# A transformer kernel on one core: the mixer's triangular inverse laid out for fewer block transposes, its elementwise work moved from GpSimd to VectorE, and a fixed queue place for one tile's transposes

## The chip, the cores and the metric

One core of a Trainium2 chip runs the whole program: TensorE (PE) does the matmuls, VectorE (DVE), ScalarE (ACT) and GpSimd (POOL) the work around them, and SyncE (SP) issues most of the transfers. The metric is the device time of one execution in microseconds (us). The kernel before was timed three times: 3140.81, 3150.64 and 3153.42 us, median 3150.64.

## The reference

The program is a stack of blocks over 512 tokens of width 1024, in float32. The change touches the first two: a hybrid mixer (a two-directional delta-rule scan over 8 heads, and a pooling branch) and a mixture over 16,384 experts (PEER). What follows them (two more attention mixers and two feed-forward layers) is untouched.

```python
def step(state, inp):                     # the scan, run forwards and backwards
    r_t, w_t, k_t, v_t, kk_t, a_t = inp
    sa = jnp.einsum('bhvk,bhk->bhv', state, -kk_t)
    state = (state * w_t[:, :, None, :]
             + sa[..., :, None] * (kk_t * a_t)[..., None, :]
             + v_t[..., :, None] * k_t[..., None, :])
    out = jnp.einsum('bhvk,bhk->bhv', state, r_t)
    return state, out

p = h @ w_in                              # the mixer: project, shift, scan, gate, pool, project
p_rw = bi_token_shift(p[..., :RWKV_IN], shift_mu)
...
y_pool = multiscale_pool(p_pool, pool_w, pool_scale)
return jnp.concatenate([y_rwkv, y_pool], axis=-1) @ w_out

ug = jnp.take(u_tab, idx, axis=0)         # the experts, for each token's 128 chosen rows
act = gelu(jnp.einsum('td,thkd->thk', xb, ug))
vg = jnp.take(v_tab, idx, axis=0)
return jnp.einsum('thk,thkd->td', gate * act, vg)
```

## The kernel before

**The mixer** (`mixer`, lines 1305 to 1484) takes roughly the first 508 us. Eight heads are worked as four pairs j = 0 to 3; a pair fills the 128 partitions, 64 for each head. The 512 tokens are cut into 8 chunks of 64, and inside a chunk the recurrence is solved in closed form: a strictly triangular 64x64 matrix is inverted for each chunk, head and direction. A pair goes through these steps:

- `keys`, `decay`, `queries` (lines 1589 to 1714) make the scaled operands: tiles `kk`, `sg`, `L`, `ta`, `b`, `BK`, `AR`, `kfs`. Much of it is elementwise on 128x512 (or 64x512) tiles, split between VectorE (`V`) and GpSimd (`G`).
- `grams` (from line 1715) multiplies them on TensorE and masks the products into `Ga` and `BG` (line 1739).
- `invert` (from line 1780) inverts the triangles. The 32x32 diagonal blocks are first transposed by VectorE into `W`, four transposes of 32 partitions each (line 1797). Then 15 rows of forward substitution run on VectorE, two small instructions for each row (lines 1810 and 1812), on all chunks at once. The 16x16 inverses and their transposes are scaled by ScalarE into `W` (line 1819) and brought back into `X` and `TT` by four transposes each (line 1824); `X` and `TT` were zeroed by GpSimd before. Two rounds of small matmuls (line 1834, results taken by lines 1842, 1847 and 1850) merge the blocks to 32 and 64.
- `solve`, `chain`, `tail` and `gate` form the outputs `y`.

The input projection runs as filler between these steps (`project`, tile `pp`): each pair of weight columns is loaded as `mraw`, and `split` turns it into two halves `mw`, one by a ScalarE cast and the other by a subtraction (lines 1524 and 1525), which goes to VectorE and to GpSimd by turns. The result is taken from PSUM and shifted by one ScalarE and two VectorE instructions (lines 1382 to 1385). The pooling branch adds on GpSimd, and the output projection splits its weights `ow` in the same way as `mw`.

The order comes from `timeline`: two tracks of pairs, (0, 2) and (1, 3), the second 69 units later, each step with a cost for each `yield`; the filler is placed behind the tracks' matmuls. A scheduler then orders each engine's instructions by when it takes them to be ready. Every engine runs its own queue in order.

**The experts.** Three of four token tiles meet all 128 expert columns densely: for each column a `pu` product of 24 matmuls and later a `pacc` sum of 18. Token tile 0 is instead worked from gathered rows (`chosen`): GpSimd issues an indirect transfer for each row and VectorE accumulates into `pe_acc` (line 634). When it is done, `end` (line 722) normalises tile 0 and `lay` (line 179) scales it into `xn` on VectorE (line 185) and transposes it on TensorE into `pf` (line 190), in the middle of the dense columns.

Of the kernel before, what the change touches and what calls it, by code (L numbers as in the profile page):

```python
# [23 lines left out]
S = 512  # L24
# [375 lines left out]
class Peer:  # L400
# [154 lines left out]
    def dense(self, wk, ps, hhi, hlo, early):  # L555
# [7 lines left out]
        def down(w, ahi, alo, i, t):  # L563
            l = [y[:, t * 128:(t + 1) * 128] for y in (ahi, alo)]
            for h in range(2):
                mm = k.mm3(acc[t][h], l, [y[:, h * 512:(h + 1) * 512] for y in w], i == 0, i == 127)
            return mm.ins
# [154 lines left out]
    def end(self, st, t, u, g, gpre, pool, ps):  # L722


        k, nc = self.k, self.k.nc
        V, A, G = nc.vector, nc.scalar, nc.gpsimd
        v = pool.tile([128, D], F32, name=k.name("v"), tag="v")
        y = pool.tile([128, D], F32, name=k.name("xn"), tag="xn")
        ms = k.small.tile([128, 2, 4], F32, name=k.name("ms"), tag="ems", bufs=2)
        for h in range(2):  # L730
            sl = slice(h * 512, (h + 1) * 512)
            d = V.tensor_tensor(out=v[:, sl], in0=u[:, sl], in1=g[:, sl], op=ALU.mult)
            for z, src in ((0, u), (1, v)):
                c = A.activation(y[:, sl], src[:, sl], AF.Square, scale=1.0 / 32.0, accum_out=ms[:, z, h:h + 1])
        st.marks.append((c.ins, d.ins))
        for _ in range(1 + 6 * (t == 0)):
            yield
        s = ms[:, :, 2]
        G.tensor_tensor(out=s, in0=ms[:, :, 0], in1=ms[:, :, 1], op=ALU.add)
        G.tensor_scalar(out=s[:, 0:1], in0=s[:, 0:1], scalar1=1e-5, scalar2=None, op0=ALU.add)  # L740
        G.tensor_scalar(out=ms[:, 0, 3:4], in0=s[:, 0:1], scalar1=1e-6, scalar2=None, op0=ALU.mult)
        G.tensor_tensor(out=s[:, 1:2], in0=s[:, 1:2], in1=ms[:, 0, 3:4], op=ALU.add)
        G.tensor_tensor(out=s, in0=s, in1=k.mhalf[:, 0:2], op=ALU.pow)
        st.lay(t, v, y, s[:, 1:2], gpre, lambda: ps.tile([128, 4, 128], F32, name=k.name("pf"), tag="pu"))
        A.activation(st.x[:, t, :], v, AF.Copy, scale=s[:, 0:1])
# [559 lines left out]
def mixer(k, ctx, xpool, a, ready):  # L1305
# [5 lines left out]
    with ExitStack() as psctx, ExitStack() as lctx:  # L1311
# [37 lines left out]
        with ExitStack() as rctx, ExitStack() as pctx:  # L1349
# [13 lines left out]
            def project(f, fin, tag="pj"):  # L1363

                p = ps.tile([128, 512], F32, name=k.name("pp"), tag=tag, bufs=1 if tag == "pj" else 3)
                for c2 in range(0, NC, 2):
# [3 lines left out]
                    split(k, raw, *w, eng=V if c2 % 4 else G)  # L1370
# [98 lines left out]
            for n, c in enumerate(order):  # L1469
                yz = part(late, 0, c, 2)  # L1470
                for h in range(2):
# [3 lines left out]
                    split(k, raw, *w, eng=G if h else V)  # L1475
# [11 lines left out]
def pool_branch(k, a, yp, col, rw, ps):  # L1487
# [7 lines left out]
    for gi, hw in enumerate(POOL_HALF):  # L1495
# [9 lines left out]
        for lv in range(gi + 1):  # L1505
            st = 1 << lv
            n -= st
            dst = q[lv % 2]
            G.tensor_tensor(out=dst[:, :n], in0=src[:, :n], in1=src[:, st:st + n], op=ALU.add)
            src = dst  # L1510
            yield
        m = rw.tl("db")
        G.tensor_tensor(out=m, in0=src[:, 16 - hw:16 - hw + S], in1=inv, op=ALU.mult)
# [41 lines left out]
class Rwkv:  # L1555
# [76 lines left out]
    def decay(self, j, d):  # L1632
# [26 lines left out]
        G.tensor_tensor(out=sg, in0=L, in1=sg, op=ALU.subtract)  # L1659
# [12 lines left out]
        else:  # L1672
            G.tensor_tensor(out=kfs, in0=kfs, in1=R(ta), op=ALU.add)
        G.tensor_tensor(out=ta, in0=ta, in1=R(kT), op=ALU.mult)
        yield
        BK = st["BK", d] = dt("BK", (128, 8, 2, 64))
        for h in range(2):
# [4 lines left out]
            G.tensor_tensor(out=BK[q, :, 1 - h, :], in0=ch(ta[q]), in1=ch(L[q]), op=ALU.mult)  # L1682
            yield

    def queries(self, j, d):
# [10 lines left out]
        G.tensor_tensor(out=AR[d][:, :, 1, :], in0=ch(R(r)), in1=e3, op=ALU.mult)  # L1696
        yield
        vd = v
        if d:
            vd = self.dt("sg")  # L1700
            G.tensor_copy(vd, v[:, ::-1])
# [13 lines left out]
    def grams(self, j, d):  # L1715
# [7 lines left out]
        if d == 0:  # L1723
            st["Ga"] = tl("Ga", (128, 2, 16, 64), 2)
        Ga = st["Ga"][:, :, 8 * d:8 * d + 8, :]
        msk = e.con("gmask").rearrange("p (s t) -> p s t", s=2)
        for c4 in range(2):
# [8 lines left out]
            for h in range(2):  # L1736
# [4 lines left out]
                yield  # L1741
        for c4 in range(2):
# [21 lines left out]
    def bonus(self, j):  # L1764
# [7 lines left out]
        G.tensor_tensor(out=kfs, in0=kfs, in1=r, op=ALU.mult)  # L1772
# [7 lines left out]
    def invert(self, j):  # L1780
# [9 lines left out]
        W = tl("W", (128, 16, 32))  # L1790
        P = tl("P", (128, 16, 64))
        tmp = P.rearrange("p a b -> p (a b)")
        Nn, Tt = (tmp[:, i * 256:(i + 1) * 256].rearrange("p (a b) -> p a b", a=16) for i in range(2))
        for h in range(2):
            for q in range(2):
                rows = slice(64 * h + 32 * q, 64 * h + 32 * q + 32)
                V.transpose(W[rows].rearrange("p a b -> p (a b)"),
                            Ga[rows, h, :, 32 * q:32 * q + 32].rearrange("p n (b t) -> p t b n", b=2))
                yield
# [14 lines left out]
        TT = tl("TT", (128, 16, 64))  # L1814
# [230 lines left out]
for _n, _c in (("blk", 128), ("gmask", 128), ("m16", 64), ("m32", 64), ("eye", 64), ("m01", 2), ("reset", 512)):  # L2045
# [25 lines left out]
def consts():  # L2071
# [10 lines left out]
    m["m01"] = np.stack([p % 32 < 16, p % 32 >= 16], 1)  # L2082
    m["reset"] = np.tile((np.arange(512) % 64 != 0)[None, :], (128, 1))
# [69 lines left out]
```

## Time and profile before

| what | value |
|---|---|
| median of three runs | 3150.64 us |
| the profiled execution | 3154.2 us, its span 3152.4 us |
| PE, DVE, ACT, POOL busy | 95%, 64%, 43%, 29% of the span |
| mean granted TensorE clock | 0.971 of full speed |

The span runs from the first to the last instruction. PE's share is the sum of modelled matmul times, so it is an upper figure. [...] The profile's share of POOL counts gathers in the expert stage too; the mixer is a sixth of the span.

### The profile page before, as it was taken

Reading aid. Unit: us, or ns where it says so; the run is one execution under the profiler, and the core shown is the slowest. Engines: PE = TensorE matmul, PEld = TensorE weight load, DVE = VectorE, ACT = ScalarE, POOL = GpSimd, SP = SyncE. Lnnn points to the kernel's source line nnn. Section 1 sums busy time; section 2 is a strip of 40 time slices with the busy share of each in tenths; the row PEclk is TensorE's granted clock in tenths of the full one; section 3 lists DMA queues with packets and bytes.
Section 4 is the critical chain, followed back from the end, with each engine's and each line's share of the span. In section 5 each row is a group of like instructions: output and inputs, shape, how many; then the busy total and the mean of one; then the engine's idle time right before and its main releaser. Section 6 shows DMA issues by size and latency. Waiting matters only on the chain. (4 is left out here: it accounts for less than half of the span.)

```text
span 3152.4 us, 45760 instructions
## 1 busy us (share of the span) xinstructions
PE 2982.1 (95%) x17602; PEld 2514.9 (80%) x17602; DVE 2030.4 (64%) x3837; ACT 1348.7 (43%) x2459; POOL 906.1 (29%) x662
## 2 busy tenths in 40 slices
PE   7888999998799999999998999989999899999999
PEld 5656668998688999999997987758888787888887
DVE  5767747998987888878887455665552343655522
ACT  5333334337733333333333355564442254544422
POOL 4322234630012544444443021212222331122221
PEclk9878999999999999999999999899999999999999
DMA  2000135234336999999997432313332332122322
GB/s 90 23 18 17 38 106 177 88 119 163 157 129 238 353 328 336 334 341 326 339 327 270 128 116 74 114 58 112 100 98 91 95 128 83 64 95 94 100 95 80
DMA packets 176202, 476.08 MB, mean 151 GB/s; under 512 B 18768, under 2 KB 68688, under 8 KB 175728
## 3 DMA queue, kind: packets, MB, share of 16 engines
q1 hardware_dynamic: 139120, 338.93, 31.8%
q0 software_dynamic: 36864, 134.23, 11.7%
q8 instruction: 138, 2.26, 0.3%
q14 instruction: 80, 0.66, 0.1%
HBM read 448.59 MB, written 24.51 MB: 150 GB/s over the span
## 5 line engine op out<-in xcount | busy, mean ns | idle before, releaser
L64 ACT CAST whi<-raw 128x1024 fp32r<-128x1024 f32 x494 | 518.1, 1050 | 712.2 <-PE pu L118 187.0
L67 DVE TENSOR_TENSOR wlo<-raw,whi 128x1024 fp32r<-128x1024 f32 x366 | 457.4, 1250 | 459.5 <-ACT whi L64 457.5
L67 POOL TENSOR_TENSOR wlo<-raw,whi 128x1024 fp32r<-128x1024 f32 x128 | 310.5, 2427 | 1085.6 <-ACT whi L64 994.3
L117 PE MATMUL pu<-pe_hhi,whi 128*128 128x384 f32 x1024 | 348.8, 341 | 2.3 <-ACT gl L545 1.7
L119 PE MATMUL pu<-pe_hhi,wlo 128*128 128x384 f32 x1024 | 347.2, 339 | 0.0
L118 PE MATMUL pu<-pe_hlo,whi 128*128 128x384 f32 x1024 | 347.1, 339 | 0.0
L118 PE MATMUL pacc<-wlo,ahi 128*128 128x512 f32 x768 | 303.3, 396 | 0.0
L117 PE MATMUL pacc<-whi,ahi 128*128 128x512 f32 x768 | 294.7, 396 | 3.1 <-ACT ahi L589 3.1
L119 PE MATMUL pacc<-whi,alo 128*128 128x512 f32 x768 | 290.7, 398 | 3.3 <-DVE alo L590 3.3
L119 PE MATMUL up<-res_h,wlo 128*128 128x512 f32 (+1 forms) x752 | 283.0, 377 | 1.0 <-DVE wlo L67 1.0
L117 PE MATMUL up<-res_h,whi 128*128 128x512 f32 (+1 forms) x752 | 283.5, 378 | 0.0
L118 PE MATMUL up<-res_h,whi 128*128 128x512 f32 (+1 forms) x752 | 283.4, 377 | 0.0
L253 DVE SCALAR_TENSOR_TENSOR u<-up,ffn_par,u 128x511 f32<-128x511 f32 (+1 forms) x176 | 131.4, 748 | 142.7 <-ACT u L251 139.6
L618 POOL DMA_INDIRECT row<-pe_v,pe_gs x128 | 165.6, 1294 | 199.4 <-DVE pe_acc L634 186.7
L618 POOL DMA_INDIRECT row<-pe_rows,pe_gs x128 | 167.0, 1305 | 189.2 <-DVE pe_gs L625 167.5
L117 PEld LDWEIGHTS pu<-pe_hhi,whi 128*128 128x128 f32 x1024 | 193.2, 189 | 7.6 <-ACT gl L545 2.0
L118 PEld LDWEIGHTS pu<-pe_hlo,whi 128*128 128x128 f32 x1024 | 193.2, 189 | 4.2
L119 PEld LDWEIGHTS pu<-pe_hhi,wlo 128*128 128x128 f32 x1024 | 192.9, 188 | 0.5
L119 PEld LDWEIGHTS pacc<-whi,alo 128*128 128x128 f32 x768 | 144.9, 189 | 38.1 <-DVE alo L590 3.8
L117 PEld LDWEIGHTS pacc<-whi,ahi 128*128 128x128 f32 x768 | 144.7, 189 | 33.4 <-ACT ahi L589 3.8
L118 PEld LDWEIGHTS pacc<-wlo,ahi 128*128 128x128 f32 x768 | 144.7, 188 | 30.9
L634 DVE SCALAR_TENSOR_TENSOR pe_acc<-row,pe_gs,pe_acc 128x1024 f32<-128x1024 f32 x128 | 163.7, 1279 | 4.0 <-DMA row<-pe_v,pe_gs 3.4
(502 smaller groups left out, 6460.2 us busy)
## 6 DMA issues: line engine op xcount, KB each, us to landing
raw<-pe_u SPq DMA_DIRECT2D x128, 512.0 KB, 5.5
raw<-pe_v SPq DMA_DIRECT2D x128, 512.0 KB, 5.8
raw<-ffn_up SPq DMA_DIRECT2D x88, 512.0 KB, 3.5
raw<-ffn_dn SPq DMA_DIRECT2D x44, 512.0 KB, 3.5
pe_gd<-go SPq DMA_DIRECT2D x24, 784.0 KB, 3.4
gc<-pe_gd SPq DMA_DIRECT2D x12, 1536.0 KB, 15.3
mraw<-mx_in SPq DMA_DIRECT2D x80, 128.0 KB, 2.2
raw<-pe_wq SPq DMA_DIRECT2D x16, 512.0 KB, 3.6
```

What stands on the lines that cost most here:

```text
L64: nc.scalar.copy(hi, raw)
L67: eng.tensor_tensor(out=lo, in0=raw, in1=hi, op=ALU.subtract)
L117: mm(out, l[0], r[0], start=first, stop=False)
L118: mm(out, l[0], r[1], start=False, stop=False)
L119: return mm(out, l[1], r[0], start=False, stop=last)
L253: V.scalar_tensor_tensor(out=u[:, d:], in0=p[:, :S - d], scalar=par[:, o + 2 - d:o + 3 - d], in1=u[:, d:], op0=ALU.mult, op1=ALU.add)
L618: G.indirect_dma_start(out=r, out_offset=None, in_=table[z], in_offset=bass.IndirectOffsetOnAxis(ap=idx[:, j:j + 1], axis=0))
L634: V.scalar_tensor_tensor(out=acc, in0=row("v", j), scalar=w[:, j:j + 1], in1=acc, op0=ALU.mult, op1=ALU.add)
```

## The change

In the inverse, ScalarE copies the 32x32 diagonal blocks of `Ga` into a compact tile `Dg`, 32 columns wide, at the end of the masking in `grams`: four copies of 32 partitions for each direction. One transpose of 128 partitions then takes the place of four. On the way back the scaled inverses `Z` are made by VectorE (they lie in `TT`), one transpose for each of `X` and `TT` writes a compact tile `Y` (in `P`), and two instructions, one on VectorE and one on ScalarE, spread it into the left and right 32 columns with a 0/1 factor (`half`) that also writes the zeros. The two memsets of `X` and `TT` on GpSimd are gone. Twelve transposes for each pair become three.

All other tensor work of the mixer on GpSimd goes to VectorE: of `decay` and `queries`, of `bonus`, the GpSimd half of the weight splits, and the pooling branch. Two memsets of the inverse stay on GpSimd. 114 instructions move.

In the experts, `lay` of token tile 0 is put behind the last `pacc` matmul written before it (`issue_after` orders TensorE's queue only, and is no wait).

On VectorE the end of the first pair's inverse stood so before (`X_864`, `TT_944` the results, `W` the source, the rows around them the masks of the next pair and a weight split):

```order
L1812 TENSOR_REDUCE P_866<-P_866 128x15
L1525 TENSOR_TENSOR mw_1168<-mraw_1165,mw_1167 128x256
L1824 STREAM_TRANSPOSE X_864<-W_946 32x16x2x16 x4
L1739 TENSOR_TENSOR Ga_1145<-rp_1146,mx_cst 128x256
L1739 TENSOR_TENSOR BG_27_213<-rp_1146,mx_cst 128x4x64
L1739 TENSOR_TENSOR Ga_1145<-rp_1147,mx_cst 128x256
L1739 TENSOR_TENSOR BG_27_213<-rp_1147,mx_cst 128x4x64
L1824 STREAM_TRANSPOSE TT_944<-W_966 32x16x2x16 x4
```

And now, from three rows before the last reduction (`ta` and `BK` were GpSimd's):

```order
L1676 TENSOR_TENSOR ta_1016<-ta_1016,mx_k_88 128x512
L1817 TENSOR_TENSOR P_884<-P_884 128x225
L1684 TENSOR_TENSOR BK_1070<-ta_1016,L_1036 64x8x64 x2
L1819 TENSOR_REDUCE P_884<-P_884 128x15
L1527 TENSOR_TENSOR mw_1096<-mraw_1093,mw_1095 128x256
L1823 TENSOR_SCALAR TT_883<-P_884,mx_cst 128x16x16 x4
L1828 STREAM_TRANSPOSE P_884<-TT_883 128x16x2x16 x2
L1830 TENSOR_SCALAR X_882<-P_884,mx_cst 128x16x32
L1527 TENSOR_TENSOR mw_1186<-mraw_1183,mw_1185 128x256
L1830 TENSOR_SCALAR TT_883<-P_884,mx_cst 128x16x32
```

Eight transposes have become two, four scalings and two spreading copies stand beside them, and the elementwise work of the next pair stands among the last rows of the substitution. The masks of the next pair come after the inverse.

On TensorE the transposes of token tile 0 (`pf`) stood so before, between the sums of one expert column and the product of the next:

```order
L119 MATMUL pacc_9086<-whi_16453,alo_16392 128x512
L119 MATMUL pacc_9087<-whi_16453,alo_16392 128x512
L190 MATMUL pf_16402<-ident,xn_16264 128x128 x4
L190 MATMUL pf_16410<-ident,xn_16264 128x128 x4
L117 MATMUL pu_16418<-pe_hhi,whi_16421 128x384
```

And now:

```order
L119 MATMUL pacc_9082<-whi_16449,alo_16388 128x512
L119 MATMUL pacc_9083<-whi_16449,alo_16388 128x512
L190 MATMUL pf_16398<-ident,xn_16260 128x128 x4
L190 MATMUL pf_16406<-ident,xn_16260 128x128 x4
L117 MATMUL pu_16414<-pe_hhi,whi_16417 128x384
```

The names are numbered otherwise; 114 of the 128 `pu` products stand ahead of `pf` in both. From the first query matmul of the experts on, TensorE's queue differs from before in one exchange of two neighbouring rows, behind `pf`; those of VectorE, ScalarE, GpSimd and SyncE are the same from the expert stage on.

```diff
@@ dense
             for h in range(2):
                 mm = k.mm3(acc[t][h], l, [y[:, h * 512:(h + 1) * 512] for y in w], i == 0, i == 127)
+            self.mark = mm.ins
@@ end
-        st.lay(t, v, y, s[:, 1:2], gpre, lambda: ps.tile([128, 4, 128], F32, name=k.name("pf"), tag="pu"))
+        with nullcontext() if t else k.tc.issue_after(self.mark):
+            st.lay(t, v, y, s[:, 1:2], gpre, lambda: ps.tile([128, 4, 128], F32, name=k.name("pf"), tag="pu"))
@@ mixer, project / output projection
-                    split(k, raw, *w, eng=V if c2 % 4 else G)
+                    split(k, raw, *w)
-                    split(k, raw, *w, eng=G if h else V)
+                    split(k, raw, *w)
@@ decay, queries, bonus, pool_branch: G becomes V, as in
-        G.tensor_tensor(out=sg, in0=L, in1=sg, op=ALU.subtract)
+        V.tensor_tensor(out=sg, in0=L, in1=sg, op=ALU.subtract)
-        G.tensor_tensor(out=ta, in0=ta, in1=R(kT), op=ALU.mult)
+        V.tensor_tensor(out=ta, in0=ta, in1=R(kT), op=ALU.mult)
-            G.tensor_tensor(out=BK[q, :, 1 - h, :], in0=ch(ta[q]), in1=ch(L[q]), op=ALU.mult)
+            V.tensor_tensor(out=BK[q, :, 1 - h, :], in0=ch(ta[q]), in1=ch(L[q]), op=ALU.mult)
...
@@ grams
+            st["Dg"] = tl("Dg", (128, 16, 32))
...
+        for h in range(2):
+            for q in range(2):
+                rows = slice(64 * h + 32 * q, 64 * h + 32 * q + 32)
+                A.copy(st["Dg"][rows, 8 * d:8 * d + 8, :], Ga[rows, h, :, 32 * q:32 * q + 32])
+            yield
@@ invert
-        for h in range(2):
-            for q in range(2):
-                rows = slice(64 * h + 32 * q, 64 * h + 32 * q + 32)
-                V.transpose(W[rows].rearrange("p a b -> p (a b)"),
-                            Ga[rows, h, :, 32 * q:32 * q + 32].rearrange("p n (b t) -> p t b n", b=2))
-                yield
+        TT, P = tl("TT", (128, 16, 64)), tl("P", (128, 16, 64))
+        Z = [TT.rearrange("p a b -> p (a b)")[:, i * 512:(i + 1) * 512].rearrange("p (a b) -> p a b", a=16) for i in range(2)]
+        Y = [tmp[:, i * 512:(i + 1) * 512].rearrange("p (a b) -> p a b", a=16) for i in (1, 0)]
+        W = Z[1]
+        V.transpose(W.rearrange("p a b -> p (a b)"), st["Dg"].rearrange("p n (b t) -> p t b n", b=2))
+        yield
...
-        for dst, src in ((X, Tt), (TT, Tt.rearrange("p a b -> p b a"))):
-            G.memset(dst, 0.0)
-            Z = tl("W", (128, 16, 32))
+        for z, src in zip(Z, (Tt, Tt.rearrange("p a b -> p b a"))):
             for b2 in range(2):
-                A.activation(Z[:, :, 16 * b2:16 * b2 + 16], src, AF.Copy, scale=m01[:, b2:b2 + 1])
-            yield
-            for h in range(2):
-                for q in range(2):
-                    rows = slice(64 * h + 32 * q, 64 * h + 32 * q + 32)
-                    V.transpose(dst[rows, :, 32 * q:32 * q + 32].rearrange("p n (b t) -> p t b n", b=2),
-                                Z[rows].rearrange("p a b -> p (a b)"))
-                    yield
+                V.tensor_scalar(out=z[:, :, 16 * b2:16 * b2 + 16], in0=src, scalar1=m01[:, b2:b2 + 1], scalar2=None,
+                                op0=ALU.mult)
+            yield
+        half = con("half")
+        for dst, z, y in zip((X, TT), Z, Y):
+            V.transpose(y.rearrange("p n (b t) -> p t b n", b=2), z.rearrange("p a b -> p (a b)"))
+            yield
+            V.tensor_scalar(out=dst[:, :, 0:32], in0=y, scalar1=half[:, 0:1], scalar2=None, op0=ALU.mult)
+            A.activation(dst[:, :, 32:64], y, AF.Copy, scale=half[:, 1:2])
+            yield
```

## Rows read from the trace of the kernel before

**Rows 1.** Stretches of the mixer: length; PE, PEld, DVE, ACT, POOL busy; clock; DMA share.

```profile
20.00:88.00 68.00, 58.54 (x365) 42.26 (x364) 37.81 (x59) 32.64 (x61) 28.63 (x30) 0.92 0.16 51
88.00:131.00 43.00, 31.77 (x243) 22.93 (x244) 39.38 (x77) 20.97 (x37) 10.52 (x10) 0.82 0.08 25
131.00:174.00 43.00, 40.64 (x722) 33.57 (x721) 25.51 (x45) 10.59 (x24) 14.69 (x15) 0.95 0.06 21
174.00:215.00 41.00, 28.47 (x272) 19.66 (x269) 36.65 (x75) 21.61 (x34) 6.25 (x6) 0.79 0.04 14
215.00:265.00 50.00, 48.58 (x702) 37.32 (x704) 30.62 (x54) 13.86 (x29) 18.73 (x18) 0.83 0.06 20
265.00:308.00 43.00, 31.06 (x362) 21.12 (x358) 36.70 (x79) 21.70 (x33) 7.89 (x7) 0.82 0.05 17
308.00:360.00 52.00, 52.00 (x790) 40.08 (x786) 30.46 (x67) 17.01 (x35) 17.41 (x17) 0.95 0.13 39
360.00:394.00 34.00, 27.34 (x171) 16.51 (x168) 28.95 (x63) 13.88 (x24) 5.26 (x6) 0.90 0.09 29
428.00:508.00 80.00, 71.90 (x489) 53.61 (x489) 46.74 (x80) 41.33 (x69) 33.11 (x27) 0.98 0.52 168
```

**Rows 2.** Waits of PE from 20 to 508 us: us in total, times, longest.

```profile
PE pp L117 <- DVE mx_v L1385: 11.4, 2, 8.1
PE rp L1834 <- DVE TT L1824: 9.2, 3, 6.6
PE rp L1928 <- DVE AV L1922: 6.0, 12, 1.3
```

**Rows 3.** Timeline of DVE at the second pair's inverse: start, us, instruction, idle before.

```profile
193.53 0.39 DVE L1812 TENSOR_REDUCE P<-P 128x15 f32<-128x225 f32 x1
195.34 4.21 DVE L1824 STREAM_TRANSPOSE X<-W 32x512 f32<-32x512 f32 x4 [1.42 <-ACT W L1819]
...
202.11 4.17 DVE L1824 STREAM_TRANSPOSE TT<-W 32x512 f32<-32x512 f32 x4
```

**Rows 4.** Groups of DVE to 508 us: busy us, mean ns, idle before.

```profile
L1525 DVE TENSOR_TENSOR mw<-mraw,mw 128x256 fp32r<-128x256 f32 x40 | 21.6, 541 | 23.8 <-ACT mw L1524 23.3
...
L1797 DVE STREAM_TRANSPOSE W<-Ga 32x512 f32<-32x512 f32 x16 | 17.1, 1069 | 0.2
L1824 DVE STREAM_TRANSPOSE TT<-W 32x512 f32<-32x512 f32 x16 | 16.8, 1050 | 1.2 <-ACT W L1819 0.9
L1824 DVE STREAM_TRANSPOSE X<-W 32x512 f32<-32x512 f32 x16 | 16.8, 1049 | 2.7 <-ACT W L1819 2.5
...
L1842 DVE TENSOR_TENSOR P<-rp,mx_cst 128x512 f32<-128x512 f32 x16 | 11.0, 687 | 9.9 <-PE rp L1834 9.9
```

**Rows 5.** Single lines: duration in ns, min/median/max.

```profile
L1525 DVE TENSOR_TENSOR mw<-mraw,mw x40: 399/425/1226, 15.5 to 411.8; 128x256 fp32r<-128x256 f32 x40
...
L1655 DVE TENSOR_SCALAR sg<-sg x8: 415/428/428, 39.0 to 324.7; 128x512 f32<-128x512 f32 x8
...
L1679 DVE SCALAR_TENSOR_TENSOR BK<-b,L x16: 670/1352/1764, 45.4 to 345.2; 64x512 f32<-64x512 f32 x16
...
L1694 DVE TENSOR_TENSOR AR<-kk,AR x8: 692/1064/1734, 43.8 to 331.4; 128x512 f32<-128x512 f32 x8
...
L1803 DVE TENSOR_SCALAR P<-P x4: 280/282/294, 94.8 to 365.9; 128x256 f32<-128x256 f32 x4
```

**Rows 6.** Groups of POOL to 508 us.

```profile
L1525 POOL TENSOR_TENSOR mw<-mraw,mw 128x256 fp32r<-128x256 f32 x40 | 31.5, 787 | 186.0 <-ACT mw L1524 185.8
L1682 POOL TENSOR_TENSOR BK<-ta,L 64x512 f32<-64x512 f32 x16 | 23.9, 1497 | 5.7 <-PE rp L1745 5.1
...
L1659 POOL TENSOR_TENSOR sg<-L,sg 128x512 f32<-128x512 f32 x8 | 11.2, 1397 | 32.6 <-DVE L L1657 32.6
```

**Rows 7.** A group of ACT to 508 us.

```profile
L1875 ACT ACTIVATE UV<-rp 64x256 f32<-64x256 f32 x16 | 6.1, 378 | 0.0
```

**Rows 8.** Timeline of PE where token tile 0 is transposed.

```profile
1724.00 1.97 PE L190 MATMUL pf<-ident,xn 128*128 128x128 f32 x8 [10.26 <-DVE xn L185]
```

More of the change, by code (lines that the diff above doesn't have):

```diff
@@ L1508, in pool_branch @@
             dst = q[lv % 2]
-            G.tensor_tensor(out=dst[:, :n], in0=src[:, :n], in1=src[:, st:st + n], op=ALU.add)
+            V.tensor_tensor(out=dst[:, :n], in0=src[:, :n], in1=src[:, st:st + n], op=ALU.add)
             src = dst
@@ L1512, in pool_branch @@
         m = rw.tl("db")
-        G.tensor_tensor(out=m, in0=src[:, 16 - hw:16 - hw + S], in1=inv, op=ALU.mult)
+        V.tensor_tensor(out=m, in0=src[:, 16 - hw:16 - hw + S], in1=inv, op=ALU.mult)
         V.tensor_tensor(out=m, in0=m, in1=pg[:, 16:16 + S], op=ALU.subtract)
@@ L1672, in decay @@
         else:
-            G.tensor_tensor(out=kfs, in0=kfs, in1=R(ta), op=ALU.add)
-        G.tensor_tensor(out=ta, in0=ta, in1=R(kT), op=ALU.mult)
+            V.tensor_tensor(out=kfs, in0=kfs, in1=R(ta), op=ALU.add)
+        V.tensor_tensor(out=ta, in0=ta, in1=R(kT), op=ALU.mult)
         yield
@@ L1695, in queries @@
         yield
-        G.tensor_tensor(out=AR[d][:, :, 1, :], in0=ch(R(r)), in1=e3, op=ALU.mult)
+        V.tensor_tensor(out=AR[d][:, :, 1, :], in0=ch(R(r)), in1=e3, op=ALU.mult)
         yield
@@ L1700, in queries @@
             vd = self.dt("sg")
-            G.tensor_copy(vd, v[:, ::-1])
+            V.tensor_copy(vd, v[:, ::-1])
         vc = ch(vd)
@@ L1771, in bonus @@
         yield
-        G.tensor_tensor(out=kfs, in0=kfs, in1=r, op=ALU.mult)
+        V.tensor_tensor(out=kfs, in0=kfs, in1=r, op=ALU.mult)
         yield
@@ L1787, in invert @@
         st["X"] = X
-        W = tl("W", (128, 16, 32))
-        P = tl("P", (128, 16, 64))
+        TT, P = tl("TT", (128, 16, 64)), tl("P", (128, 16, 64))
         tmp = P.rearrange("p a b -> p (a b)")
         Nn, Tt = (tmp[:, i * 256:(i + 1) * 256].rearrange("p (a b) -> p a b", a=16) for i in range(2))
-        for h in range(2):
-            for q in range(2):
-                rows = slice(64 * h + 32 * q, 64 * h + 32 * q + 32)
-                V.transpose(W[rows].rearrange("p a b -> p (a b)"),
-                            Ga[rows, h, :, 32 * q:32 * q + 32].rearrange("p n (b t) -> p t b n", b=2))
-                yield
+        Z = [TT.rearrange("p a b -> p (a b)")[:, i * 512:(i + 1) * 512].rearrange("p (a b) -> p a b", a=16) for i in range(2)]
[3 more added lines that the diff above has]
+        yield
         m01 = con("m01")
@@ L1813, in invert @@
             yield
-        TT = tl("TT", (128, 16, 64))
-        for dst, src in ((X, Tt), (TT, Tt.rearrange("p a b -> p b a"))):
-            G.memset(dst, 0.0)
-            Z = tl("W", (128, 16, 32))
+        for z, src in zip(Z, (Tt, Tt.rearrange("p a b -> p b a"))):
             for b2 in range(2):
-                A.activation(Z[:, :, 16 * b2:16 * b2 + 16], src, AF.Copy, scale=m01[:, b2:b2 + 1])
+                V.tensor_scalar(out=z[:, :, 16 * b2:16 * b2 + 16], in0=src, scalar1=m01[:, b2:b2 + 1], scalar2=None,
+                                op0=ALU.mult)
             yield
-            for h in range(2):
-                for q in range(2):
-                    rows = slice(64 * h + 32 * q, 64 * h + 32 * q + 32)
-                    V.transpose(dst[rows, :, 32 * q:32 * q + 32].rearrange("p n (b t) -> p t b n", b=2),
-                                Z[rows].rearrange("p a b -> p (a b)"))
-                    yield
+        half = con("half")
[5 more added lines that the diff above has]
+            yield
         def pairmm(l, rr, fin):
@@ L2044 @@
 MC_OFF, MC_N = {}, 0
-for _n, _c in (("blk", 128), ("gmask", 128), ("m16", 64), ("m32", 64), ("eye", 64), ("m01", 2), ("reset", 512)):
+for _n, _c in (("blk", 128), ("gmask", 128), ("m16", 64), ("m32", 64), ("eye", 64), ("m01", 2), ("half", 2), ("reset", 512)):
     MC_OFF[_n] = (MC_N, _c)
@@ L2082, in consts @@
     m["m01"] = np.stack([p % 32 < 16, p % 32 >= 16], 1)
+    m["half"] = np.stack([s < 32, s >= 32], 1)
     m["reset"] = np.tile((np.arange(512) % 64 != 0)[None, :], (128, 1))
```

## The prediction

> **What bounds the kernel now.** I read the busy table by stage first, then TensorE's waits, then the timeline of VectorE inside one wait, then the groups of each engine. Behind the mixer nothing moves on any queue, so only its 508 us count. There the table shows two kinds of stretch [rows 1]. In four of them (88 to 131, 174 to 215, 265 to 308 and 360 to 394 us), one for each pair's inverse, PE is busy for 31.8, 28.5, 31.1 and 27.3 us and so idle for 11.2, 12.5, 11.9 and 6.7 us, 42 in all. Its granted clock is 0.82, 0.79, 0.82 and 0.90, while VectorE is busy for 85 to 92%. Between them PE is busy for 40.6 of 43, 48.6 of 50 and 52 of 52 us, and VectorE for only 59 to 61%. So the mixer's time is the sum of stretches that VectorE sets and stretches that PE sets. TensorE's longest waits agree: for VectorE's evacuation of the projection (11.4 us, one of 8.1) and for `TT` (9.2 us, one of 6.6) [rows 2]. In the second pair's inverse the last row of the substitution ends at 193.9 us, the first four transposes start after a further wait for ScalarE at 195.3 and the last end at 206.3 us: 12.4 us in which PE has next to nothing [rows 3].
>
> **Removed: 36 of 48 transposes.** A transpose of 32 partitions takes 1.05 us in all three places [rows 4]. A pair has twelve, 12.6 us; now three. The form with 128 partitions is not in the trace. Its bounds are 1.05 us (the same row length, the partitions side by side) and 4.2 us (four blocks one after the other, the four that it replaces) [rows 3, 4]. I take 1.05, the row of one instruction with as many columns, and get -9.45 us for a pair; at the other end the gain is nil.
>
> [...] The sum goes by the row.
>
> **Added in the same chain.** Four scalings of 128x256 on VectorE at 0.28 us and two spreading copies of 128x512 at 0.43 us [rows 5]: +2.0 us for a pair. The ScalarE halves of the spreading run beside the next transpose. The wait for ScalarE's scaling ahead of the first transpose, 1.42 us in the second pair [rows 3], goes: -1.4. In exchange the first transpose waits for the last copies into `Dg`; ScalarE's nearest form, 64x256, takes 0.38 us [rows 7], the copies before the last two lie beside VectorE's masks, so +0.8.
>
> **Moved: 114 instructions from GpSimd to VectorE.** Uncontended, a two-input instruction of this size takes 0.67 to 0.69 us on VectorE [rows 4, 5] against 1.40 to 1.60 on GpSimd [rows 6], and a weight split 0.40 against 0.79. All of it is 48 x 0.69 + 40 x 0.40 + 26 x 0.69 (8 output splits, 4 copies and 14 of pooling, priced alike) = 67 us more for VectorE over the mixer. In the stretches between the inverses VectorE is idle for 17, 19 and 22 us [rows 1], which covers its share there at nothing. If that cover were gone, each would cost its own length. Inside the first inverse's stretch the new order has five such instructions ahead of the end of the inverse (`sg`, `AR`, `ta`, two `BK`): +3.5 us for a pair.
>
> **Given back: contention.** VectorE's instructions are stretched while GpSimd works: `BK` has a minimum of 0.67 and a median of 1.35 us, `AR` 0.69 and 1.06, the weight split a minimum of 0.40 and a mean of 0.54 [rows 4, 5]. With GpSimd silent I expect the minimum: 16 x 0.68 + 8 x 0.37 + 40 x 0.14 = 19.4 us over the mixer. Its bounds are zero (the stretching has another cause) and the 19.4. I put half in the inverses' stretches: -2.5 us for a pair.
>
> **The sum.** A pair's inverse: -9.45 + 2.0 - 1.4 + 0.8 + 3.5 - 2.5 = -7.05 us. Three stretches have over 11 us of idle PE and can take it whole, -21.2. The fourth has 6.7 us, so -6.7. The operands of the first pair (20 to 88 us, 9.5 us of PE idle [rows 1]) lose the slower engine in their chain: in each direction two `BK` instructions on GpSimd, 1.5 us each [rows 6], and one before them become half as long, partly beside PE's work: -3. The output projection (428 to 508 us, 8 idle) loses a few waits for GpSimd's splits: -1. In all -32. What stays in the stretches however fast the inverse is, such as PE's 6.0 us for the chain's `AV` [rows 2], hardly yields. I take 2 off for it. So -30 of the profiled execution's 3154.2 us (3152.4 of span, 1.8 around it), 3124.2. That execution was 3.6 us above the median, and the forecast is 3150.6 - 30 = 3121 us.
>
> **The gathered tile.** PE waits 10.3 us for `xn` ahead of `pf` [rows 8]. The new code fixes the place of `pf` behind the last `pacc` before it, and the queue shows it behind the 114th `pu` product before and now. So I price it at zero: the wait stays, and what gathers and accumulates ahead of it is queued as before. The bounds are 0 and -10.3, if the stage should run in with more slack; I have no row for that.
>
> **Late next.** With the inverse's tail shortened, the 15 rows of substitution, the `AV` chain and the projection's evacuation on VectorE are what PE waits for; these are unchanged, and VectorE stays the bound of those stretches.
>
> **Rivals.**
> 1. VectorE's queue is blocked at its head. On GpSimd 40 weight splits waited 186 us for ScalarE's casts and 8 `sg` waited 33 [rows 6]; that cost nothing, since little was behind them. On VectorE the 40 that are there already wait 23.8 us, 0.6 each [rows 4]. If the 52 moved ones that follow a cast or an exponential wait as long, 31 us are lost and the gain is gone; from there on the kernel is slower. At twice that, 1.2 us each, 62 are lost against some 31 gained: 3182 us. For it: in the second inverse splits stand among the substitution's rows. Against it: a split that waits for ScalarE mostly waits when VectorE has nothing else, and its busy share leaves 40% free outside the inverses. [...]
> 2. PE takes up only half. The filler and the pairs' small matmuls are put in order by times that the scheduler assumed; where a stretch of VectorE gets 7 us shorter, PE may meet the next wait (`u`, `AV`, a cast) instead. Then half of 32, 3135 us. For it: TensorE's waits are many and short, besides the two large ones [rows 2].
> 3. The clock comes back too. The four stretches ran at 0.79 to 0.90, and the one from 215 to 265 us at 0.83 although PE was busy throughout [rows 1]: the clock fell while PE had waited. Full clock there would give 0.17 x 50 = 8.5 us, and in the three long inverses 7.7, 8.6 and 7.7 us (the missing share of the clock times the length), of which I count 10, since VectorE sets much of them. Together -30 - 8.5 - 10 = -48, 3102 us. Against it: VectorE remains the bound and PE still waits in the inverses. [...]
> 4. The wide transpose costs as much as the four narrow ones. Then -9.45 drops out of each pair, +2.4 is left of its sum, 9.6 for four pairs against the 4 saved elsewhere: 3156 us, no change that can be told.
>
> **How the numbers follow.** A measurement of this kernel tells from no change what is beyond about 0.5%, 15.8 us: faster is below 3134.9, slower above 3166.4. The forecast (gain of 20 to 42 us) has 0.54, rival 3 0.10, rival 2 (gain of 8 to 20) 0.19, rival 4 0.04, rival 1 0.13, of which 0.03 ends within 0.5%. Faster: 0.54 + 0.10 + 0.07 of rival 2 = 0.71. Slower: 0.10. Within: 0.12 + 0.04 + 0.03 = 0.19. The range leaves out gains over 52 us (0.03 of rival 3) and what ends above 3148 (rivals 1 and 4, 0.17): 3098 to 3148 us. The forecast's own range is 3109 to 3131.
>
> **What would show it.** Right: STREAM_TRANSPOSE of 128x512 near 1.05 us, twelve of them; `BK` and `AR` on VectorE near 0.69 us with hardly any spread; POOL next to silent until the experts; the inverses' stretches 6 to 9 us shorter with VectorE still above 80% in them; the first query matmul of the experts some 30 us earlier, and every later stage as long as before, `pf` with its 10 us wait included. Wrong: waits of VectorE for ScalarE's casts of well over 24 us and PE idle behind them (rival 1); the same idle PE under new names (rival 2); a wide transpose of several us (rival 4); or a stage behind the mixer that changes its length.

## The result, and the profile after

The changed kernel takes 3105.8 us (median of four runs, 3101.2 to 3106.0) against 3149.0 of the kernel before: ratio 0.9857, 95% interval 0.9833 to 0.9881, so 37 to 53 us less. The forecast was 3121, 15 us too high. The profiled execution took 3105.84 us, its span is 3104.1 and its mean clock 0.981.

The gain lies ahead of the experts: 44.0 us there, of 48.3 us by which the span is shorter. (The profiled execution of before was 5 us above its median.) These are the mixer and the stages behind it, before and then after (length; PE, PEld, DVE, ACT, POOL busy; clock; DMA share):

```profile
20.00:508.00 488.00, 423.30 (x4557) 311.59 (x4555) 325.67 (x616) 203.07 (x367) 150.08 (x141) 0.90 0.18 58
508.00:820.00 312.00, 287.00 (x2074) 278.89 (x2073) 283.44 (x912) 161.30 (x452) 102.80 (x67) 0.99 0.35 123
820.00:1710.00 890.00, 877.40 (x4361) 781.29 (x4360) 734.83 (x1115) 334.35 (x539) 352.28 (x272) 1.00 0.84 301
1740.00:3152.00 1412.00, 1365.73 (x6496) 1118.95 (x6494) 663.43 (x1162) 629.43 (x1067) 293.27 (x164) 0.98 0.30 96
```

```profile
20.00:464.00 444.00, 399.33 (x4575) 295.26 (x4573) 323.52 (x718) 212.16 (x391) 15.17 (x18) 0.95 0.19 63
464.00:776.00 312.00, 286.55 (x2066) 277.92 (x2064) 285.66 (x916) 162.97 (x456) 102.82 (x67) 0.99 0.36 126
776.00:1666.00 890.00, 878.00 (x4357) 782.23 (x4357) 733.59 (x1112) 334.26 (x534) 350.98 (x272) 1.00 0.84 300
1696.00:3104.00 1408.00, 1361.02 (x6491) 1114.59 (x6489) 662.54 (x1161) 629.95 (x1067) 293.53 (x164) 0.98 0.30 96
```

Shifted by 44 us, the later stages are alike: the same PE busy time in each within 5 us (the last was cut 4 us shorter). The first query matmul starts at 458.0 instead of 502.0 us. In the mixer PE's idle time fell by 20 us (64.7 to 44.7), and its busy time by 24 us, with the same products: they ran at a clock of 0.95 instead of 0.90.

Cut at each pair's first transposes and at the first mask behind its inverse, the mixer after reads (same columns):

```profile
85.07:115.18 30.11, 21.32 (x208) 15.25 (x207) 28.24 (x72) 17.23 (x29) 0.00 (x0) 0.83 0.11 36
115.18:161.79 46.61, 45.74 (x787) 37.14 (x784) 32.08 (x71) 16.24 (x36) 0.44 (x2) 1.00 0.06 19
161.79:191.57 29.78, 20.49 (x196) 13.82 (x195) 26.05 (x67) 19.95 (x30) 0.00 (x0) 0.80 0.06 18
191.57:238.95 47.38, 45.81 (x771) 35.95 (x769) 33.25 (x71) 17.66 (x38) 0.44 (x2) 0.98 0.07 22
238.95:271.78 32.83, 24.21 (x295) 15.81 (x293) 24.36 (x69) 18.04 (x26) 0.00 (x0) 0.95 0.07 21
...
325.11:349.79 24.68, 20.65 (x154) 10.90 (x150) 20.07 (x56) 11.91 (x19) 0.00 (x0) 0.93 0.04 12
349.79:464.00 114.21, 109.55 (x964) 80.71 (x963) 72.76 (x136) 51.78 (x95) 13.85 (x12) 1.00 0.48 156
```

These answer [rows 1]. Cut in the same way, the four inverses of the kernel before read:

```profile
88.27:131.12 42.85, 31.62 (x244) 23.04 (x245) 39.10 (x76) 21.09 (x37) 10.64 (x10) 0.81 0.08 25
173.67:211.12 37.45, 25.57 (x240) 17.89 (x240) 33.14 (x72) 19.04 (x29) 3.15 (x3) 0.77 0.05 15
261.85:302.75 40.90, 31.38 (x365) 20.92 (x363) 34.59 (x77) 21.06 (x33) 4.03 (x5) 0.87 0.06 17
359.61:394.93 35.32, 28.66 (x208) 17.75 (x206) 30.09 (x65) 14.27 (x24) 5.26 (x6) 0.90 0.10 30
```

They took 42.9, 37.5, 40.9 and 35.3 us. Now they are 30.1, 29.8, 32.8 and 24.7: 39.1 us less. The start is 3.2 us shorter. All that lies between and behind the inverses lost 1.7 us together: the first gap became 4.1 us longer and the stretch behind the last inverse 1.1, the other two gaps 3.4 and 3.5 shorter. A cut between two such stretches is no border for the work: of PE's matmuls, 853 lie in the four inverses now where 1057 lay, and some 200 more between and behind them. VectorE is still busy for 94, 87, 74 and 81% of the inverses (over 80% was forecast; the third misses it).

VectorE's groups from 20 to 480 us answer [rows 4, 5] (busy us, mean ns, idle before):

```profile
L1527 DVE TENSOR_TENSOR mw<-mraw,mw 128x256 fp32r<-128x256 f32 x78 | 32.5, 420 | 29.6 <-ACT mw L1526 29.3
L1817 DVE TENSOR_TENSOR P<-P 128x1 f32<-128x1 f32 (+14 forms) x60 | 17.6, 293 | 1.6
L1681 DVE SCALAR_TENSOR_TENSOR BK<-b,L 64x512 f32<-64x512 f32 x16 | 11.0, 684 | 0.7 <-PE rp L1753 0.5
L1828 DVE STREAM_TRANSPOSE P<-TT 128x512 f32<-128x512 f32 x8 | 7.8, 1050 | 0.0
L1696 DVE TENSOR_TENSOR AR<-kk,AR 128x512 f32<-128x512 f32 x8 | 5.5, 688 | 0.7 <-ACT AR L1669 0.6
L1823 DVE TENSOR_SCALAR TT<-P,mx_cst 128x256 f32<-128x256 f32 x16 | 5.2, 392 | 0.0
L1805 DVE STREAM_TRANSPOSE TT<-Dg 128x512 f32<-128x512 f32 x4 | 4.4, 1095 | 2.7 <-ACT Dg L1748 2.7
```

The wide transpose takes 1.05 us, what the narrow one took. `BK`, `AR` and the split take 684, 688 and 420 ns in the mean, near what was their minimum (670, 692 and 399 [rows 5]). PE's longest waits of the mixer answer [rows 2] (us, times, longest):

```profile
PE pp L117 <- DVE mx_v L1387: 11.2, 2, 8.3
PE rp L1840 <- DVE TT L1830: 7.6, 2, 7.1
PE rp L1840 <- DVE P L1848: 6.9, 3, 5.7
```

And this is the end of the second pair's inverse on VectorE, which answers [rows 3]:

```profile
179.56 1.30 DVE L1823 TENSOR_SCALAR TT<-P,mx_cst 128x256 f32<-128x256 f32 x4
180.77 0.42 DVE L1657 TENSOR_SCALAR sg<-sg 128x512 f32<-128x512 f32 x1
181.10 1.91 DVE L1828 STREAM_TRANSPOSE P<-TT 128x512 f32<-128x512 f32 x2
...
185.56 0.48 DVE L1830 TENSOR_SCALAR X<-P,mx_cst 128x512 f32<-128x512 f32 x1
185.96 0.74 DVE L1385 SCALAR_TENSOR_TENSOR mx_v<-pp,mx_par,mx_v 128x511 f32<-128x511 f32 x1
186.62 0.48 DVE L1830 TENSOR_SCALAR TT<-P,mx_cst 128x512 f32<-128x512 f32 x1
```

From the start of the scalings to the last VectorE part of `TT` it takes 7.5 us, where 12.4 us lay between the last row and the last transpose before. Four other instructions stand in the gap. Token tile 0's transposes wait as they did in [rows 8], 45.6 us earlier:

```profile
1678.45 1.97 PE L190 MATMUL pf<-ident,xn 128*128 128x128 f32 x8 [10.28 <-DVE xn L185]
```

### The profile page after: what moved, and what is told of

Read it like the earlier page. It is cut to its first block, busy times and chain, and to the rows that moved or that the text cites. A ratio compares the mean times of both kernels' runs of the same rounds, so it can differ in the third digit from the quotient of the medians.

```text
span 3104.1 us, 45731 instructions
## 1 busy us (share of the span) xinstructions
PE 2952.8 (95%) x17602; PEld 2493.7 (80%) x17602; DVE 2027.9 (65%) x3939; ACT 1359.3 (44%) x2483; POOL 768.8 (25%) x540
```

## The experiments

Every ratio is against the kernel before on the same chip; "gain" is that ratio on 3149 us. The medians come from several chips, so a difference of two medians can be some us off the difference of the gains.

| kernel | median us | ratio, 95% interval | gain |
|---|---|---|---|
| the change | 3105.8 | 0.9857 (0.9833 to 0.9881) | 45 |
| transposes alone | 3126.0 | 0.9928 (0.9914 to 0.9943) | 23 |
| all work off GpSimd alone | 3138.8 | 0.9968 (0.9955 to 0.9982) | 10 |
| splits alone | 3142.5 | 0.9982 (0.9970 to 0.9993) | 6 |
| elementwise alone | 3128.4 | 0.9936 (0.9922 to 0.9951) | 20 |
| change, splits back | 3110.2 | 0.9883 (0.9862 to 0.9904) | 37 |
| change, GpSimd reads | 3129.8 | 0.9946 (0.9927 to 0.9964) | 17 |
| change, GpSimd writes | 3106.9 | 0.9874 (0.9854 to 0.9895) | 40 |
| before, added products | 3155.1 | 1.0014 (1.0003 to 1.0025) | -4 |
| change, added products | 3138.0 | 0.9967 (0.9955 to 0.9979) | 10 |
| change, no fixed place | 3106.2 | 0.9859 (0.9844 to 0.9874) | 44 |
| change, `pf` later | 3099.6 | 0.9845 (0.9826 to 0.9863) | 49 |
| `pf` later, closed tail | 3107.4 | 0.9857 (0.9831 to 0.9884) | 45 |

**The parts, one at a time.** The compact transposes alone: the edits of `grams` and `invert` as in the change, all `G` kept.

> Before, with the compact tiles of the inverse alone (three wide transposes for twelve narrow ones); all elementwise work and the splits stay on GpSimd by turns as before. Theory T (the terms of the prediction, with the part of the silent GpSimd larger than given there): the inverse of a pair loses 9.45 - 2.0 + 1.4 - 0.8 = 8.05 us, times four less what PE can't take up, so 27 to 31 us below before, 3118 to 3122 us. Rival P (what the changed kernel gained beyond the prediction, and most of the rest, comes from GpSimd's silence alone): at most 15 us gained, 3134 or more. Rival X (the transposes gave all of it): 40 us or more, 3109 or less.

The gain was 23 us, below theory T's 27 to 31 and outside both rivals' ranges. From the first transposes to `TT` the four inverses shrank from 136.0 to 90.8 us, 45 us, more than the sum had given. But 20 us came back between them; PE's matmuls in the four inverses went from 1057 to 789, so part of the work had only moved into the gaps. The third gap, 56.9 us before and 53.3 in the change, here is

```profile
274.83:346.79 71.96, 61.79 (x921) 46.36 (x919) 43.57 (x84) 32.13 (x60) 21.72 (x19) 0.90 0.10 28
```

with GpSimd busy for 22 us and PE idle for 10.

All work off GpSimd, with the old transposes:

```diff
-        G.tensor_tensor(out=sg, in0=L, in1=sg, op=ALU.subtract)
+        V.tensor_tensor(out=sg, in0=L, in1=sg, op=ALU.subtract)
...
-                    split(k, raw, *w, eng=V if c2 % 4 else G)
+                    split(k, raw, *w)
```

> Before, with all tensor work moved from GpSimd to VectorE and the old twelve transposes. Theory T: first operands -3, output projection -1, and in the four inverses the moved work (+3.5 each) against the full contention relief (-5 each) and what the clock gives back: 10 to 15 us below before, 3134 to 3139 us. Rival P: 30 us or more gained, 3119 or less. Rival X: within 5 us of before, or slower, since VectorE has 67 us more to do.

3138.8, inside theory T's range. Then its two halves by themselves, the `split` lines first and then the others.

> Before, with the weight splits alone moved from GpSimd to VectorE (52 of the 114 instructions, with those of the output projection); the elementwise work of decay, queries, bonus and pooling stays on GpSimd. Theory T: splits on VectorE meet less contention (40 x 0.14 = 5.6 us over the mixer) and cost 16 us of VectorE time, mostly under PE's stretches: between 5 us faster and 5 us slower than before. Rival Q (the head of the queue: a split that waits for a cast holds up what is behind it): slower by 10 us or more, and the wait of VectorE for casts over 45 us against 23.

> Before, with the elementwise work (decay, queries, bonus, pooling) alone moved from GpSimd to VectorE; half of the weight splits stay on GpSimd. Theory T: the instructions of twice the length leave the chains of the operands (-3) and the contention of BK, AR and b goes (about -14 of 19 us, part of it in the inverses), against 3.5 us more in a pair's inverse: 5 to 12 us faster than before. Rival Q: no gain, since the moved instructions wait for exponentials at the head of VectorE's queue.

The splits gained 6 us, just over theory T's 5, but not for its reason: a split took 594 ns on VectorE in the mean, against 541 before, so the splits met no less contention. (48 splits moved, 40 and 8 of the output projection, not 52.) The elementwise work alone gained 20, well above theory T's 5 to 12, and 10 more than both halves together. VectorE's waits for the splits' casts differ by about as much, all work moved first, the elementwise work alone second (us, times, longest). That they are where the 10 us went is likely and not shown:

```profile
DVE mw L1525 <- ACT mw L1524: 22.8, 23, 4.6
```

```profile
DVE mw L1525 <- ACT mw L1524: 11.2, 11, 2.3
```

The elementwise move does not shorten the inverse (139.0 us to `TT` against 136.0). It shortens the three gaps between a pair's first mask and the next pair's first transposes: 43.5, 36.0 and 52.6 us against 42.5, 50.7 and 56.9, 18 us in all. So each half of the change works on another stretch: the transposes shorten the inverses, and the work off GpSimd keeps the gaps from giving that back. 23 and 10 make 33, and together they gave 45.

The change with the splits back on GpSimd:

> The changed kernel with the weight splits alone given back to GpSimd (every second pair of columns, and one half of the output projection's), as before. In the kernel with the old transposes, moving the elementwise work alone gained 20 to 21 us and moving the splits as well only 10 to 11, so there the splits on VectorE cost 10. Theory S (the cost is VectorE's time and its waits for casts, and carries over): 3094 to 3100 us, 6 to 12 below the changed kernel. Rival H (in the shortened inverse the contention that the splits bring back is worth as much as their time on VectorE): 3102 to 3116 us, with the substitution's products at 300 ns or more and BK, AR and b stretched again in part.

3110.2: theory S fell. The intervals of this and of the change overlap, so what the splits cost with the old transposes isn't found here. Without the moved splits the parts simply add up (23 and 20, and 37 measured, within the intervals). What depends on the rest is the price of the splits: moving them gained 6 us in the kernel before and cost 10 once the elementwise work had moved. Rival H had the time right, and its stretching only in small part: the products at 306 ns against 293, `BK` at 738 against 684, `AR` and `b` as in the change.

**Is it GpSimd's reading?** A load that nothing needs, in each pair's inverse:

```diff
+        jk, dg = tl("jk", (128, 12, 32)), st["Dg"][:, 0:12, :]
+        for _ in range(18):
+            G.tensor_tensor(out=jk, in0=dg, in1=dg, op=ALU.mult)
         for t in range(1, 16):
```

> The changed kernel with a load on GpSimd that nothing needs: 18 products of two SBUF operands of 128x384 in each pair's inverse, about 1.05 us each, into a tile of their own. Theory C (GpSimd that reads SBUF stretches VectorE's instructions with two SBUF operands): the substitution's products go from 292 to 380 ns or more in the mean, mw, BK, AR, sg and ta there to between 1.5 and 2.5 times their length, each inverse 4 to 8 us longer, 3120 to 3138 us in all; transposes, reductions, scans and the evacuations from PSUM stay as long as they are. Rival (the stretching before had another cause): within 4 us of the changed kernel, 3102 to 3110.

The other has one such product and then `for _ in range(50): G.memset(jk, 0.0)`.

> The changed kernel with a load on GpSimd that hardly reads: one product of 128x384 and then 50 memsets of the same tile in each pair's inverse, about 0.4 us each, so about as long in all as the load of 18 products. Theory C (it is GpSimd's reading that contends): within 5 us of the changed kernel, the substitution's products at 300 ns or less. Rival (any work of GpSimd on SBUF contends): as with the products, 3120 us or more.

By the medians, the reading load cost 24 us and the writing one 1; by the ratios 28 and 5, where the interval of the writing one overlaps with the change's. The load, and the substitution's products under it, with reads and then with writes:

```profile
L1817 POOL TENSOR_TENSOR jk<-Dg 128x384 f32<-128x384 f32 x72 | 61.1, 848 | 159.3 <-ACT Dg L1748 154.0
L1820 DVE TENSOR_TENSOR P<-P 128x1 f32<-128x1 f32 (+14 forms) x60 | 34.7, 578 | 1.6
```

```profile
L1818 POOL MEMSET jk<- 128x384 f32 x200 | 85.1, 426 | 11.5
L1821 DVE TENSOR_TENSOR P<-P 128x1 f32<-128x1 f32 (+14 forms) x60 | 17.7, 294 | 1.6
```

The timeline of VectorE under the reads, where GpSimd ran from 84.0 to 100.9 us, tells the kinds apart:

```profile
87.03 0.80 DVE L1810 TENSOR_SCALAR P<-P 128x256 f32<-128x256 f32 x1
87.94 0.67 DVE L1820 TENSOR_TENSOR P<-P 128x1 f32<-128x1 f32 x1
...
88.86 0.14 DVE L1822 TENSOR_REDUCE P<-P 128x1 f32<-128x1 f32 x1
89.03 0.61 DVE L1820 TENSOR_TENSOR P<-P 128x4 f32<-128x4 f32 x1
89.56 0.74 DVE L1385 SCALAR_TENSOR_TENSOR mx_r<-pp,mx_par,mx_r 128x511 f32<-128x511 f32 x1
```

A product of a single column took 0.67 us, most of one GpSimd instruction (0.85), and 0.16 in the change. The first reduction, with one input, and the instruction with one large operand in PSUM took 0.14 and 0.74 us, as in the change (0.15 and 0.74). Theory C holds for the products, 578 ns in the mean against 293 in the change and 294 under the writes; of the four splits beside this load one took 1.01 us and three 0.41. Not only instructions with two SBUF operands were stretched: the scaling of line 1810, with one, took 0.80 us instead of 0.29. And `BK`, `AR`, `sg` and `ta`, which the theory also named, stayed at 0.68, since they came when the load was over (in this inverse from 105.0 us on).

**Is it TensorE's clock?** Products that nothing needs keep PE busy in the inverse, in the kernel before and in the changed one:

```diff
+            if t in (6, 9, 12, 15):
+                T.matmul(wm[0:16, 0:16], Tt[:, t, :], Tt[:, t, :], start=True, stop=True)
+                for _ in range(2):
+                    T.matmul(wm, con("blk"), con("reset"), start=True, stop=True)
```

> The kernel before, with products that nothing needs put into TensorE's queue in each pair's inverse: behind rows 6, 9, 12 and 15 of the substitution a 16x16 product that reads the row, and two of 128x512 in float32 from constants, about 1 us each, some 8 us for a pair; VectorE's work is as before. Theory K (a good part of what the mixer loses is TensorE's lower clock after it has stood idle in the inverse: in the rows of before it is at 0.50 to 0.54 from 215 to 235 us although it is busy all that time): the granted clock from 20 us to the experts rises from 0.90 to 0.94 or more, and the time falls by 5 to 15 us, 3132 to 3142. Rival L (VectorE sets these stretches whatever the clock, and the products only stand in the way): 0 to 15 us slower than before.

> The changed kernel with the same products in TensorE's queue behind rows 6, 9, 12 and 15 of each pair's substitution. Theory K: the clock from 20 us to the experts rises from 0.95 to 0.98 and the time falls by 3 to 10 us, 3096 to 3103. Rival L: the idle stretches that are left are short and the products delay what is queued behind them: 3106 to 3115.

The stretch from 20 us to 6 us behind the first query matmul (columns as above), and then the added products (groups), in the kernel before:

```profile
20.00:507.20 487.20, 437.24 (x4666) 309.65 (x4666) 326.01 (x616) 202.12 (x367) 150.35 (x140) 0.95 0.19 59
```

```profile
L1817 PE MATMUL rp<-mx_cst 128*128 128x512 f32 x64 | 34.7, 667 | 0.0
L1815 PE MATMUL rp<-P 128*16 128x16 f32 x32 | 3.5, 184 | 6.5 <-DVE P L1813 6.5
```

And the same two views of the changed kernel with them:

```profile
20.00:493.80 473.80, 431.78 (x4662) 308.58 (x4661) 328.74 (x716) 211.54 (x391) 17.04 (x18) 0.96 0.19 59
```

```profile
L1824 PE MATMUL rp<-mx_cst 128*128 128x512 f32 x64 | 33.5, 648 | 0.0
L1822 PE MATMUL rp<-P 128*16 128x16 f32 x32 | 3.5, 184 | 4.5 <-DVE P L1820 4.5
```

In the kernel before, the clock rose from 0.90 to 0.95 as theory K had it, and the needed products took 437.2 - 38.2 = 399.0 us instead of 423.3, as little as in the changed kernel. (The profiled execution took 3144.7 us, the shortest of eleven with a median of 3155.1, so its clock is on the high side.) Yet the time did not fall; it is 4 us longer, as rival L had it. That doesn't show that the clock is worth nothing. At the first mask behind the third inverse this kernel was 18.7 us ahead of the kernel before, and the gap behind it took 17.3 back (the kernel before, then with the added products):

```profile
302.75:359.61 56.86, 54.44 (x822) 42.36 (x823) 35.28 (x72) 18.25 (x38) 22.00 (x20) 0.91 0.12 38
284.05:358.24 74.19, 65.68 (x898) 48.82 (x896) 43.98 (x86) 31.99 (x57) 24.16 (x22) 0.91 0.12 32
```

PE is idle for 8.5 us there, and 898 matmuls lie in the gap instead of 822: the same gap grew as with the transposes alone. In the changed kernel the clock rose only to 0.96, and 37 us of added work cost 32 (35 by the ratios), more than either theory gave. PE's idle time hardly fell, from 44.7 to 42.0 us, so the products found next to no room that they could use. A limit of this pair: what the higher clock gave, what the added work took and what the new order did can't be parted in one run.

**The gathered tile.** The change without the fixed place (the `with nullcontext() ...` and `self.mark` lines left out):

> The changed kernel without the fixed place of token tile 0's transposes. They stand behind the 114th product of the dense columns in TensorE's queue with it and without it, and the wait of 10.3 us is there in either. Theory N (the second part of the change does nothing): within 3 us of the changed kernel, 3103 to 3109 us, pf waits 10.3 us. Rival: the order of the sums ahead of pf, which differs, is worth something: more than 5 us off.

3106.2 and a wait of 10.28 us at 1678.9: theory N. Then `end` written six steps later:

```diff
-        for _ in range(1 + 6 * (t == 0)):
+        for _ in range(1 + 12 * (t == 0)):
```

> The changed kernel with the normalisation of token tile 0 written six steps later, so that its transposes stand behind two more expert columns in TensorE's queue (84 matmuls at about 0.2 us, 17 us later). Theory W (the 10.3 us wait ahead of pf is nothing but the chain of pe_acc, the squares, the root and xn, which runs beside other work if PE comes later): the wait goes, 3094 to 3098 us. Rival: part of it comes back behind pf (the evacuation of pf, and the casts and the product that wait for a bank), 3099 to 3106 us.

```profile
1686.47 1.03 PE L190 MATMUL pf<-ident,xn 128*128 128x128 f32 x8
```

The wait is gone, and the last `pf` matmul, that of the last token tile, comes 11 us earlier in the profile (1806.5 against 1817.7), but the span is only 4.0 us shorter. The median is 3099.6, just inside the rival's range, and the intervals overlap with the change's. So the wait ends as theory W says, and a gain of 6 us by the medians, 4 by the ratios, isn't shown.

**A last version.** The same with the `yield`s between scalings, transposes and spreading copies removed, for the four instructions seen above in the second pair's tail.

> The changed kernel with token tile 0's transposes two columns later and, in the inverse, no step between the scalings, the two wide transposes and the spreading copies, so that other tracks' work isn't planned between them (in the changed kernel's second pair four other VectorE instructions, 3.4 us, stand between the second transpose's end and the spread of TT). Theory F (what stands between them is only moved up into the substitution, and PE, where 37 us of added work cost 32, is what bounds the mixer now): within 5 us of the version with the later transposes alone, 3094 to 3105 us. Rival G (VectorE's tail still sets the stretch): each pair's merge starts 2 to 4 us earlier and the kernel is 7 us or more faster, under 3093 us.

3107.4 (3094.8 to 3111.3): no gain, so rival G falls. It is 2 us above theory F's range, and 8 us above the version with the later transposes alone where theory F allowed 5; the intervals overlap. That version has the lowest median of all that ran, 3099.6 us, 1.5% below the kernel before, not clearly below the changed one.

## Why the prediction was right, and where its size was off

Its main claim held: the mixer's inverses shorten because VectorE's tail does, and no later stage changes. It gave 30 us and 44 came. Step by step:

- **The reading.** Two slips that moved nothing: in the 12.4 us at the end of the second inverse PE was busy for 4.4 us, so not "next to nothing", and [rows 6] has 1.40 to 1.50 us for GpSimd's instructions, not 1.60.
- **Transposes.** Right. The 128-partition form takes 1.05 us on the way back and 1.10 from `Dg`, near the lower bound that I took, and rival 4 falls.
- **Added in the chain.** Nearly right. The scalings take 0.39 us instead of 0.28, the spreading copies 0.45 to 0.48, the first transpose waits 0.7 us for `Dg` (0.8 given), and the waits ahead of `X` and `TT` are gone. From the first transposes to `TT` the four inverses went from 136.0 to 92.9 us. Of that, VectorE's time for the inverse's own instructions lost 32.8 us (84.1 to 51.3, each counted from where the one before it ended); the terms -9.45 and +2.0 give 29.8.
- **Moved work and contention.** Mis-sized. I put +3.5 into each inverse and took half of the relief, -2.5, so 4 us more over the four. By the same count other work in the inverses went from 36.9 to 34.2 us, 2.7 less: the order put at least as much out as it took in. The relief came in full: `BK`, `AR` and `b` take 684, 688 and 684 ns in the mean now, where they took 1223, 1157 and 1068, and the substitution's own products, which I had not counted, went from 326 to 293 ns in the mean. What this half of the change does by itself is to shorten the gaps, where I had priced the cover at nothing (18 us with the elementwise work alone).
- **VectorE's waits in the inverses.** Mis-sized: I gave -1.4 and +0.8 for a pair, 2.4 us over the four. VectorE's idle time from the first transposes to `TT` fell from 15.0 to 7.3 us.
- **The sum.** This is where the size was lost: -21.2 for three pairs and -6.7 for the last, 27.9 us, and 12.7, 7.7, 8.1 and 10.6 were measured, 39.1 (two of the four outside the 6 to 9 that I had named as a sign). The cap at PE's idle time took only 0.35 us off the last pair, so it isn't what failed in the number; the three terms above were 15 us too small together (43.2 us to `TT` against 28.2), and 4 came back between `TT` and the first mask. The 2 us that I took off for what hardly yields were not lost. But the picture behind the cap, that a stretch shortens by PE's idle time, is wrong: PE's idle time in the inverses fell by 8.6 us (39.3 to 30.7), and the rest of their 39.1 is busy time, in good part because some 200 matmuls moved out of the inverses. Over the whole mixer PE's idle time fell by 20 us, less than the 30 of the forecast, and the 24 us of busy time that went with the higher clock stood in no term of it. The two misses go against each other, so it is in part luck that the forecast came as near as it did.
- **First operands and output projection.** -3 given, 3.2 measured; -1 given, and 1 us longer behind the last first mask.
- **The gathered tile.** Right, zero: same place, same 10.28 us.

Of the rivals, the blocked queue (1) shows at most in small part: in the old kernel, moving the splits cost 10 us once the elementwise work had moved, and VectorE waited 11.6 us longer for casts. VectorE's waits for casts went from 23.8 us [rows 4] to 29.6 in the change, not by the 31 us from which it decides. Rival 2 falls: 44 us were gained, not 8 to 20. Rival 3 had the number, 3102, closer than the forecast, and the clock did come back: 0.83 from 215 to 265 us [rows 1] is 0.98 in the stretch that answers to it. That stretch lost 3.4 us, not 8.5, but it holds 771 matmuls now and held 682 before.

One more number on record bears on rival 3. The 53 executions of the kernel before that were timed beside the experiments differ in their mean granted clock (0.970 to 0.978), and their times go with it: 1.8 us less for each 0.001 (correlation -0.89). The four executions of the changed kernel average 0.9815 against 0.9743. By that slope I estimate that 13 of the 44 us go with the clock, about what came beyond the forecast. This is a correlation and no experiment: the clock rose along with VectorE's shorter path, no run raises the clock of the changed kernel without giving PE more to do, and the run that raises it in the kernel before changes the order too. So how much of the 14 us the clock caused stays open.

## What to carry to other kernels

When two engines set stretches by turns, price a stretch together with the gap behind it: work moves from one to the other, and a gain in one can come back in the next, as 20 of 43 us did with the transposes alone. Don't take the other engine's idle time for the measure of the gain: at another clock its busy time changes as well, here by 24 us for the same products (at 0.95 instead of 0.90). Before moving work off GpSimd, count the VectorE instructions that run beside it, the tiny ones too (here the substitution's products, 326 ns in the mean before and 293 after), and look for the gain where the moved chain stood, not only where the contention is. A fixed place in a queue does nothing until it is another place. A load of useless products shows how much room PE has, but it also moves other work, so read its stretches and not only its time.

## What the runs showed of the hardware

- Beside GpSimd's products of 128x384 (0.85 us each) VectorE's substitution products took 578 ns in the mean, and 293 in the change without this load: 0.67 and 0.16 us for one column, 0.61 and 0.36 for 121 columns, but 0.22 and 0.21 for 36.
- Beside GpSimd's memsets of 128x384 (0.43 us each) the same products took 294 ns, and the 128x256 scalings of the inverse, with one SBUF input, 521 against 392 ns in the change. Beside GpSimd's products another such scaling took 0.80 us instead of 0.29.
- A STREAM_TRANSPOSE of 512 float32 columns took 1.05 to 1.07 us in the mean on 32 partitions and 1.05 to 1.10 on 128.
- The same products took TensorE 423.3 us in the mixer at a mean granted clock of 0.90 and 399.3 at 0.95. In the gap behind the second inverse of the kernel before, PE was busy for 3.6 us from 215 to 220 us, at a clock of 0.76 (not yet at 0.50 to 0.54, as an expectation above has it). From there to 235 us the clock was 0.50 to 0.54 although PE was busy throughout, and from 235 to 240 us it was 1.00. In the changed kernel PE was busy for 0.1 us from 180 to 185 us; the clock was 0.50 from 185 to 190 us, 0.69 to 195 and 1.00 to 210.
